# Two chained matmuls with a gelu between them: half of the first and the whole of the second from seven half-size products each, five of the seven in float32r

## The chip, the cores and the metric

One core of one Trainium2 chip. The metric is the time of one execution in microseconds on the device. Runs come with a state, slow or fast, from their clock and their time. A kernel is always timed beside runs of the kernel before on the same chip.

Names: PE is TensorE (PEld its weight loads), DVE is VectorE, ACT is ScalarE.

## The reference

```python
m, k, n, p = 1024, 1024, 2048, 1024          # a: m x k, b: k x n, c: n x p, all float32
h = np.matmul(a, b)
h = 0.5 * h * (1 + np.tanh(np.sqrt(2 / np.pi) * (h + 0.044715 * h ** 3)))
return np.matmul(h, c).astype(np.float32)
```

## The kernel before

It holds h transposed (hT, with n on the partitions), so that the second matmul can take it as weights. a is turned by TensorE. The rows of a come in two halves, aT[0] and aT[1], of 512 columns each. Everything is bf16 and accumulates in float32 banks of 128 x 512.

```python
# opening: k-slices of a's early half and of b's first 768 columns, as they land
for k in range(KT):
    ...                                       # cast, four transposes, copy to aT[0][:, k]
    if k > 0:
        mm0(k - 1)                            # six tiles, accumulated over k
mm0(KT - 1)
...
def mm1(t, h):                                # one tile of hT: 8 matmuls, then the gelu
    p = ppool.tile([128, H], F32, name="ps")
    for k in range(KT):
        nc.tensor.matmul(p, b_sb[:, k, ts(t, 128)], aT[h][:, k, :],
                         start=(k == 0), stop=(k == KT - 1))
    gelu(t, h, p)
...
for mt in range(MT):                          # second matmul: 16 matmuls a tile, copy, store
    ...
        for t in range(NT):
            nc.tensor.matmul(p, hT[h][:, t, ts(j, 128)], c_sb[:, t, ds(q0, w)], ...)
        store(mt, q0, w, p)
```

## Time and profile before

| what | value |
|---|---|
| median of 3 runs at the time of the prediction | 133.43 us |
| span in the profile | 130.9 us |
| matmuls of 128 x 128 x 512 (or the same in halves) | 512 |
| their pace, bf16 | 0.2158 us at 512 columns, 0.109 at 256 |
| TensorE / VectorE / ScalarE busy | 91% / 16% / 21% |

The prediction shows how these are read: TensorE is full, the other two engines stand idle. One view it does not show is the list of waits (engine and line, what it waited for, us in total, times, longest), here for TensorE in the kernel before:

```profile
PE pt L94 <- DVE ab L91: 3.9, 4, 1.9
PE pt L149 <- DMA ab<-in_a_dram: 2.3, 1, 2.3
...
PE ps L127 <- DMA b_sb<-in_b_dram: 0.4, 1, 0.4
```

After the opening TensorE waits only 2.7 us in all, for loads. Nothing in the kernel before makes it wait for VectorE or ScalarE once the opening is over.

### The profile page before, as it was taken

The numbers are of one execution on the slowest core, as the hardware profiler recorded it, in microseconds if no ns is written. First come the engines' busy times: TensorE is split into PE (matmuls) and PEld (weight loads), VectorE is DVE, ScalarE is ACT, GpSimd is POOL, SyncE is SP. The second block draws the span as 40 slices with busy tenths as digits, with TensorE's granted clock in tenths as the row PEclk, the third lists the DMA queues.
The fourth block names the chain that finished last, engine by engine and source line by source line (L and its number), as shares of the span: only waits on it lengthen the run. The fifth ranks groups of instructions, "written<-read, shape, count | busy, mean of one in ns | idle before, by whom it ended". The sixth has DMA issues, their size and how long they took to land.

```text
span 130.9 us, 1420 instructions
## 1 busy us (share of the span) xinstructions
PE 119.2 (91%) x591; PEld 56.3 (43%) x602; DVE 21.0 (16%) x38; ACT 27.2 (21%) x50; POOL 14.6 (11%) x27
## 2 busy tenths in 40 slices
PE   6856899998299999999999999999999999999990
PEld 2323444443155444444444444444444444444570
DVE  0223451000042200000000022222222222211121
ACT  4045556516111333333333100000000000000000
POOL 2000099232462000000000000000000000000000
PEclk9999999999999999999999999999999999999999
DMA  3999999999999999950000022221111222222231
GB/s 110 201 367 380 378 236 168 179 202 205 209 211 210 211 212 211 211 112 1 0 0 0 5 80 80 80 78 59 60 59 69 80 80 80 80 80 80 80 120 40
DMA packets 12196, 17.37 MB, mean 133 GB/s; under 512 B 800, under 2 KB 6688, under 8 KB 12192
## 3 DMA queue, kind: packets, MB, share of 16 engines
q0 software_dynamic: 5952, 7.87, 34.8%
q1 hardware_dynamic: 6240, 9.44, 20.8%
q8 instruction: 4, 0.07, 0.2%
HBM read 20.97 MB, written 4.19 MB: 192 GB/s over the span
## 4 chain that ended last, share of the span: by engine, by line
PE 70%; DMA 18%; POOL 5%; SPq 4%; issue 1%; DVE 0%
PE ps L171 42%; PE ps L127 26%; DMA ab<-in_a_dram 10%; DMA b_st<-in_b_dram 7%; POOL b_sb L110 4%; SPq L66 3%; PE pt L149 1%; SPq L60 1%; DVE ot L163 0%; POOL gate L75 0%
## 5 line engine op out<-in xcount | busy, mean ns | idle before, releaser
L171 PE MATMUL ps<-c_sb,hT 128*128 128x512 bf16 (+1 forms) x267 | 55.2, 367 | 0.3
L127 PE MATMUL ps<-aT,b_sb 128*128 128x512 bf16 x172 | 38.8, 379 | 0.6 <-DMA b_sb<-in_b_dram 0.4
L171 PEld LDWEIGHTS <-hT 128*128 128x128 bf16 x272 | 26.6, 98 | 28.9
L127 PEld LDWEIGHTS <-b_sb 128*128 128x128 bf16 x176 | 16.9, 98 | 20.5 <-DMA b_sb<-in_b_dram 0.9
L103 ACT ACTIVATE hT<-ps 128x512 bf16<-128x512 f32 x30 | 17.3, 602 | 30.0 <-PE ps L127 27.7
L163 DVE COPY ot<-ps 128x512 f32<-128x512 f32 (+1 forms) x17 | 11.2, 660 | 73.2 <-PE ps L171 73.2
L86 PE MATMUL ps<-aT,b_sb 128*128 128x512 bf16 x47 | 11.5, 379 | 0.1
L97 ACT ACTIVATE b_sb<-b_st 128x384 bf16<-128x384 f32 x16 | 7.5, 515 | 10.7 <-DMA b_st<-in_b_dram 10.5
L94 PE MATMUL pt<-ident,ab 128*128 128x128 bf16 x32 | 3.4, 233 | 3.9 <-DVE ab L91 3.9
L137 POOL DMA_DIRECT2D c_sb<-in_c_dram x8 | 5.7, 714 | 6.9 <-DMA b_sb<-in_b_dram 4.7
L86 PEld LDWEIGHTS <-b_sb 128*128 128x128 bf16 x48 | 4.4, 98 | 4.0
L150 DVE COPY aT<-pt 128x1024 bf16<-128x1024 bf16 x4 | 2.8, 692 | 20.5 <-PE pt L149 20.5
L110 POOL DMA_DIRECT2D b_sb<-in_b_dram x8 | 6.0, 775 | 0.0
L80 PE MATMUL pt<-warm 128*128 128x512 bf16 x10 | 4.5, 632 | 1.2 <-DVE warm L46 1.2
L94 PEld LDWEIGHTS <-ab 128*128 128x128 bf16 x32 | 2.3, 104 | 6.9 <-DVE ab L91 5.8
L118 PE MATMUL ps<-aT,b_sb 128*128 128x512 bf16 x16 | 4.8, 379 | 0.1
L118 PEld LDWEIGHTS <-b_sb 128*128 128x128 bf16 x32 | 3.1, 98 | 3.8
L91 DVE CAST ab<-a_st 128x512 bf16<-128x512 f32 x8 | 3.6, 445 | 6.2 <-DMA a_st<-in_a_dram 6.2
L118 PE MATMUL pt<-aT,b_sb 128*128 128x512 bf16 x15 | 4.5, 379 | 0.0
L149 PE MATMUL pt<-ident,ab 128*128 128x128 bf16 x32 | 2.5, 220 | 2.3 <-DMA ab<-in_a_dram 2.3
L95 DVE COPY aT<-pt 128x512 bf16<-128x512 bf16 x8 | 3.4, 425 | 6.4 <-PE pt L94 6.4
L149 PEld LDWEIGHTS <-ab 128*128 128x128 bf16 x32 | 2.0, 98 | 3.5 <-DMA ab<-in_a_dram 2.8
(13 smaller groups left out, 7.5 us busy)
## 6 DMA issues: line engine op xcount, KB each, us to landing
c_sb<-in_c_dram POOLq DMA_DIRECT2D x8, 512.0 KB, 15.3
out_dram<-ot SPq DMA_DIRECT2D x15, 256.0 KB, 2.0
b_st<-in_b_dram SPq DMA_DIRECT2D x8, 384.0 KB, 8.7
a_st<-in_a_dram SPq DMA_DIRECT2D x3, 512.0 KB, 8.9
b_sb<-in_b_dram POOLq DMA_DIRECT2D x4, 384.0 KB, 11.4
b_sb<-in_b_dram POOLq DMA_DIRECT2D x4, 256.0 KB, 5.9
ab<-in_a_dram POOLq DMA_DIRECT2D x4, 256.0 KB, 13.8
a_st<-in_a_dram SPq DMA_DIRECT2D x2, 256.0 KB, 4.2
```

The lines of the kernel that those rows point to most:

```text
L80: nc.tensor.matmul(wps, warm[:, 0:128], warm, start=True, stop=True)
L86: nc.tensor.matmul(ps[t], b_sb[:, k, ts(t, 128)], aT[0][:, k, :], start=(k == 0), stop=(k == KT - 1))
L94: nc.tensor.transpose(pt[:, ts(j, 128)], ab[:, j, :], ident)
L97: nc.scalar.activation(b_sb[:, k, ts(i, W0 // 2)], b_st[k][:, ts(i, W0 // 2)], AF.Copy)
L103: nc.scalar.activation(hT[h][:, t, :], p, AF.Gelu_apprx_tanh)
L110: nc.gpsimd.dma_start(out=b_sb[:, k0:k0 + kn, ds(n0, w)], in_=bv[:, k0:k0 + kn, ds(n0, w)])
L118: nc.tensor.matmul(ps[t], b_sb[:, k + i, ds(W0 + t * 128, 128)], aT[0][:, k + i, :], start=(k + i == 0), stop=(k + i == KT - 1))
L127: nc.tensor.matmul(p, b_sb[:, k, ts(t, 128)], aT[h][:, k, :], start=(k == 0), stop=(k == KT - 1))
L137: nc.gpsimd.dma_start(out=c_sb[:, t0:t0 + 2, :], in_=cv[:, t0:t0 + 2, :])
L149: nc.tensor.transpose(pt[:, k, :], ab[:, ts(k, 128)], ident)
L163: nc.vector.tensor_copy(ot[:, 0:w], p)
L171: nc.tensor.matmul(p, hT[h][:, t, ts(j, 128)], c_sb[:, t, ds(q0, w)], start=(t == 0), stop=(t == NT - 1))
```

## The change

The intent is to do fewer matmuls. A product of 2 x 2 blocks takes eight block products in the plain way and seven in this one, at the price of sums of blocks:

```
S1 = A21+A22  S2 = S1-A11   S3 = A11-A21  S4 = A12-S2
T1 = B12-B11  T2 = B22-T1   T3 = B22-B12  T4 = T2-B21
C11 = A11 B11 + A12 B21                            (products 1 and 2)
V   = A11 B11 + S2 T2       U = V + S3 T3          (products 6 and 7)
C22 = U + S1 T1             C12 = V + S1 T1 + S4 B22        (products 5 and 3)
C21 = U - A22 T4                                   (product 4)
```

The sums are kept in float32r, a four-byte type for TensorE; the operands of products 1 and 2 stay bf16. The first 1024 columns of b are still done plainly (128 matmuls), the others by seven products of 16 matmuls; the second matmul by seven of 32. Below, "the first seven" and "the second seven" are these two. The diff, cut to its core:

```diff
+    class Seven:
+        def dve(self, dst, x, y, op, n=1):            # a sum, in n pieces
+            ...
+                nc.vector.tensor_tensor(out=dst[:, r], in0=x[:, r], in1=y[:, r], op=op)
+        ...
+        def plain(self, n=1):                         # B22 and -A22 as float32r, on ScalarE
+            ...
+    def seven(w, done, between):
+        ...
+        for j in range(4):
+            w.product(px[j], A11, B11, j, True)
+            p1[j] = snap("m", px[j], "p1")            # ScalarE saves the bank
+        between(1)
+        for j in range(4):
+            p = bank(Y[j])
+            w.product(p, A12, B21, j, True)
+            done(0, 0, j, plus(p, p1[j]))             # VectorE adds the saved tile
+        between(2)
+        ...                                           # product 6 onto px -> v; between(6)
+        ...                                           # product 7 onto px -> u; between(7)
+        py = [bank(i) for i in Y]
+        for j in range(4):
+            w.product(py[j], w.s[0], w.t[0], j, True)
+            done(1, 1, j, plus(py[j], u[j]))
+        between(5)
+        for j in range(4):
+            w.product(py[j], w.s[1], w.t[2], j, False)
+            done(0, 1, j, plus(py[j], v[j]))
+        between(3)
+        ...                                           # product 4 onto px
+    def between1(n):                                  # VectorE's sums in the first seven
+        if n == 2:
+            one.s3()
+        elif n == 6:
+            two.s3(2)
+            one.s4()
+            one.t4()
+        elif n == 7:
+            one.plain()
+            two.t1(4)
+        elif n == 5:
+            two.t[1] = slot("x0", [128, 8, H], F32R, "x2")
+            two.t2(4)
+    ...
+    def between2(n):                                  # and in the second
+        if n == 1:
+            two.s1(4)
+        elif n == 2:
+            two.s2(4)
+            two.t3(4)
+        elif n == 6:
+            two.s4(4)
+        elif n == 7:
+            two.plain(4)
+            two.t4(4)
```

Also changed: the opening makes seven tiles in place of six, from slices of 1024 columns of b; a's late half is loaded before b's late half, and its transposes (`turn`) and its product with b's first half come right after the opening, the first four tiles at 256 columns a matmul; 8 warm-up matmuls in place of 10. In the traces here VectorE's instructions stand in the order of the program, so the place of a sum in `between` is its place in VectorE's queue.

## The prediction

> **What bounds the kernel now.** I read the page's table of shares first, then the slices, the groups of instructions with their shapes kept apart, and the chain of work that ended last; after them the timeline of VectorE in the second matmul and of the opening.
>
> ```profile
> span 130.9 us, 1420 instructions
> PE 119.2 (91%) x591; PEld 56.3 (43%) x602; DVE 21.0 (16%) x38; ACT 27.2 (21%) x50; POOL 14.6 (11%) x27
> PE   6856899998299999999999999999999999999990
> DMA  3999999999999999950000022221111222222231
> PE 70%; DMA 18%; POOL 5%; SPq 4%; issue 1%; DVE 0%
> ```
>
> TensorE is full from about 20 us to the end, and it is 70% of the chain; VectorE and ScalarE are busy 16% and 21%. DMA is full until about 58 us of the span and then only stores. The rest of the chain (DMA, POOL, SP queue) is the loading at the front. So only fewer matmuls, or a shorter opening, can make this kernel faster.
>
> ```profile
> L171 PE MATMUL ps<-c_sb,hT 128*128 128x512 bf16 x235 | 51.7, 379 | 0.3
> L163 DVE COPY ot<-ps 128x512 f32<-128x512 f32 x15 | 10.4, 692 | 70.8 <-PE ps L171 70.8
> L171 PE MATMUL ps<-c_sb,hT 128*128 128x256 bf16 x32 | 3.7, 273 | 0.0
> L163 DVE COPY ot<-ps 128x256 f32<-128x256 f32 x2 | 0.8, 424 | 2.4 <-PE ps L171 2.4
> L171 PEld LDWEIGHTS <-hT 128*128 128x128 bf16 x272 | 26.6, 98 | 28.9
> ```
>
> A matmul's 379 ns is a latency, not a pace: the matmuls overlap. The pace stands in the copies, each of which waits for 16 matmuls:
>
> ```profile
> 75.79 0.69 DVE L163 COPY ot<-ps 128x512 f32<-128x512 f32 x1 [32.12 <-PE ps L171]
> 79.24 0.69 DVE L163 COPY ot<-ps 128x512 f32<-128x512 f32 x1 [2.76 <-PE ps L171]
> ...
> 124.14 0.69 DVE L163 COPY ot<-ps 128x512 f32<-128x512 f32 x1 [2.76 <-PE ps L171]
> 125.88 0.42 DVE L163 COPY ot<-ps 128x256 f32<-128x256 f32 x1 [1.05 <-PE ps L171]
> ```
>
> From 75.79 to 79.24 is 3.45 us for 16 matmuls: 0.2158 us each at 512 columns. From 124.14 to 125.88 is 1.74 us for 16 at 256 columns: 0.109 us. The weight load's 98 ns hides in both. The kernel has 512 full-width matmuls, 110.5 us of the span.
>
> [...] I [...] take the 0.2158 us of bf16 for it. No instruction of the kernel before shows this. [...] The trace agrees for copies: 692 minus 424 ns over 256 columns is 1.05 ns[...]. It has no two-tensor operation.
>
> **The change part by part.**
>
> Removed: the first 1024 columns of the first matmul stay as they are (128 matmuls). The other half becomes seven products of 16 in place of 128 (112), the second matmul seven of 32 in place of 256 (224). That is 464 for 512: 48 x 0.2158 = 10.4 us less TensorE work. Two of each seven products stay bf16; five take float32r, in all 5 x 16 + 5 x 32 = 240 matmuls.
>
> The opening: seven tiles in place of six, b in slices of 1024 columns. Up to b's last slice 6.29 MB must land in place of 5.24. Between 9.1 and 16.0 us the kernel before landed 2.62 MB, 378 GB/s, so 1.05 MB more costs 2.8 us; larger packets at the front should give back some 0.7. In the kernel before, the last slice was cast near 20 us and the opening matmuls ended at 22.6, with 48 done. Now the last lands about 21.5 and 56 are done at about 23.8. Eight more matmuls are worth 1.7 us, so this is roughly even. The late half of a is now loaded first, and the wait of 2.3 us for it (and 0.9 us for b) goes. Two waits for the transposed copy (0.69 us each and its hand-over) come. From 23.8: 8 matmuls 1.7, four transposes of a 1.8, 64 at 256 columns 7.0, 32 at 512 6.9, waits 2.0: the plain half ends at T0 = 43.2 us.
>
> Added on VectorE: eight sums a matmul, each with a float32r output[...]. In the first matmul one is 2048 columns: [...] 2.2 us. In the second it is 4096, in four pieces: [...] 4.6 us. An addition of a PSUM tile to a saved one is 512 columns: 0.61 us, 12 of them per matmul. After T0 there remain the sums s3, s4, t4 of the first matmul (6.6), all eight of the second (36), 24 additions (14.6) and the last copies (2): about 60 us of VectorE beside 72.5 us of TensorE (336 x 0.2158). So VectorE is no longer idle, and its order decides. The sums t3, t1, t2 come before b's late half and hide before T0; s1 and s2 end at 43.7.
>
> In the first seven products (3.45 us each), the second product's additions end at T0 + 7.7, as the matmuls do with their last 0.6. Then, in program order, VectorE has s3 2.2, the second matmul's s3 4.4, s4 and t4 4.4, the second matmul's t1 4.6: T0 + 23.3. Only then comes the first addition of product 5, which must free its bank before product 3 may write there: T0 + 24.0. TensorE is ready at T0 + 17.3. **Wait of 6.8 us.** Then the rest of these additions, t2 of the second matmul (4.6) and product 3's additions: T0 + 32.7; the gelus queue behind them on ScalarE (0.5 to 0.6 each), and the banks that the second matmul begins with are free only at T0 + 34.1. TensorE has ended product 4 at T0 + 31.0. **Wait of 3.1 us.** The second seven begin at 77.3.
>
> There, product 6 needs s2, which stands in VectorE's queue behind the additions of product 2 (last at 91.9) and comes in quarters of 1.14 us; TensorE uses a quarter in 0.43. Waits 2.1 + 3 x 0.7 = **4.2 us.** The rest of VectorE's work then fits. Without waits TensorE would end at 43.2 + 72.5 = 115.7; with 6.8 + 3.1 + 4.2 it ends at 129.8. The kernel before had its last matmul end at 127.6 and its span 3.3 us later; the same tail gives a span of 133.1. The median is 2.5 us over the span before (133.43 to 130.9): 135.6. ScalarE gains 24 savings of tiles at about 0.5 us and the plain copies of 1.9 us twice and about 1.0 us eight times, some 24 us, and stays below TensorE.
>
> **The rivals.** First, the saving arrives: the sums hide and the end is 115.7 + 1 + 3.3 + 2.5, about 122.5. For it speak that VectorE's total of 60 us is below TensorE's 72.5, and that somebody placed the sums by hand; the order I worked out would be harmless if the sums took half as long. Against it: outputs of four bytes[...]. In favour of a mild form, a few waits could be shorter than I have them: 128 to 131.
>
> Second, float32r costs more. If its weight load does not hide, each of 240 matmuls grows. At 15 ns that is 3.6 us, of which a part lies in waits that exist anyway: about 138. At 50 ns about 144. At half rate, 240 x 0.216 = 52 us less what the waits swallow: over 170. The 98 ns under 216 speak against, since even a doubled load would fit; that it is a new operand type speaks for.
>
> Third, the clock. The trace's first ten matmuls start 0.43 us apart, half the later pace[...] some 2 us lost. Nearly all of that would lie in the 3.1 us of wait that follows, so the end moves little.
>
> **Range and chances.** The mechanism gives 135.6 if float32r is free. A mild miss of the waits to the good is as likely as a small cost of float32r, so I predict 135.5. Sums of 2.0 or 2.4 us instead of 2.2 move it by about 2 us, the opening by 1, float32r by up to 6: 129.5 to 141. Two per cent are 2.7 us: faster is under 130.8, slower over 136.1. The middle lies just below the upper boundary. Faster 0.16: needs waits under 9 us in all. Same 0.42. Slower 0.42, because float32r can only cost.
>
> **What would show each step.** In the changed profile: product spacing of 3.45 us in float32r as in bf16, from the saves on ScalarE; VectorE's sums of about 2.3 us (2048) and 1.2 us (1024) in the record; an idle time of TensorE near 60 to 67 us put down to VectorE's additions, another near 74 to 77 put down to a gelu, and a broken row near 91 to 97 with matmuls waiting for s2 in quarters; VectorE busy near 75% overall and near 95% between 47 and 77. TensorE's slices should read 9 up to 60 and dip after. Wrong would be: sums at half the time (then 122), float32r matmuls more than 10 ns apart from bf16 (then 138 and up), or the late half of a landing after 25 us, which would shift everything.

## The result, and the profile after

The changed kernel took 139.19 us (median of 4 runs, 137.92 to 139.44) against 133.78 for the kernel before in the same rounds. The ratio is 1.0405, 95% interval 1.0323 to 1.0488: slower. A ratio here is the mean time of one kernel's fast runs over that of the other's of the same rounds, so not quite the quotient of the medians. It takes all four runs of the kernel before as fast; as three of them lie where later sittings have only slow ones, 1.04 is probably too low. Against fast runs alone, in a later sitting, the ratio was 1.052 (after_again, below). The output is correct. Measured again in a later sitting it had 138.98 us.

The head of its page, with the rows of TensorE, VectorE and the granted clock in 40 slices of 3.43 us, and the chain of work that ended last by engine:

```profile
span 137.2 us, 1506 instructions
PE 118.3 (86%) x570; PEld 78.4 (57%) x576; DVE 84.1 (61%) x91; ACT 50.4 (37%) x77; POOL 12.3 (9%) x23
PE   6798899797999999980399899965999999999980
...
DVE  0326443407999089999999950459959963444421
...
PEclk9999999999999999999559999999599999999998
...
PE 75%; DVE 13%; issue 5%; DMA 3%; ACT 2%; DVEq 0%
```

TensorE's row now has a hole at slices 18 and 19, counted from 0 (62 to 68 us), and a dent at 26 and 27; VectorE reads 9 before and across the hole; the clock reads 5, half speed, in two slices at the end of the hole and after it, and in one after the dent. VectorE has entered the chain with 13%. The waits of TensorE in the changed kernel:

```profile
PE ps L188 <- DVE ot L215: 6.2, 1, 6.2
PE ps L188 <- DVE s L151: 2.8, 3, 2.1
...
PE ps L188 <- ACT ot L305: 0.5, 1, 0.5
...
PE ps L188 <- ACT hT L97: 0.3, 1, 0.3
```

L188 is the products, L151 the sums, L215 the additions to saved tiles. VectorE's timeline across the hole (start, duration, instruction, count, and in brackets the idle time before it):

```profile
51.15 2.28 DVE L151 TENSOR_TENSOR x<-b 128x2048 fp32r<-128x2048 bf16 x1
53.35 4.49 DVE L151 TENSOR_TENSOR s<-hT,hT 128x2048 fp32r<-128x2048 bf16 x2
57.76 2.28 DVE L151 TENSOR_TENSOR x<-b,x 128x2048 fp32r<-128x2048 bf16 x1
59.96 2.28 DVE L151 TENSOR_TENSOR x<-x,aT 128x2048 fp32r<-128x2048 f32 x1
62.16 4.62 DVE L151 TENSOR_TENSOR x<-c_sb 128x1024 fp32r<-128x1024 bf16 x4
66.70 2.47 DVE L215 TENSOR_TENSOR ot<-ps,u 128x512 f32<-128x512 f32 x4
69.10 4.62 DVE L151 TENSOR_TENSOR x<-c_sb,x 128x1024 fp32r<-128x1024 bf16 x4
73.64 2.47 DVE L215 TENSOR_TENSOR ot<-ps,v 128x512 f32<-128x512 f32 x4
```

In order these are s3, the second matmul's s3, s4, t4, the second matmul's t1, the additions of product 5, the second matmul's t2, the additions of product 3. VectorE has no idle time here. TensorE is through with product 5 at 61.3; the first of the additions that free its bank is the one at 66.70:

```profile
67.53 9.46 PE L188 MATMUL ps<-x,x 128*128 128x512 f32 x32 [6.19 <-DVE ot L215]
77.31 1.02 PE L188 MATMUL ps<-c_sb,hT 128*128 128x512 bf16 x3 [0.32 <-ACT hT L97]
```

Products 3 and 4 then take 9.46 us; at full clock the same 32 matmuls took 7.42 (in e_best, below). The dent is product 6 of the second seven, which waits for s2 in quarters:

```profile
91.38 0.69 DVE L215 TENSOR_TENSOR ot<-ps,p 128x512 f32<-128x512 f32 x1 [1.03 <-PE ps L188]
91.98 4.62 DVE L151 TENSOR_TENSOR s<-s,hT 128x1024 fp32r<-128x1024 f32 x4
...
93.35 0.70 PE L188 MATMUL ps<-x,s 128*128 128x512 f32 x2 [2.06 <-DVE s L151]
...
94.39 0.73 PE L188 MATMUL ps<-x,s 128*128 128x512 f32 x2 [0.34 <-DVE s L151]
```

Its first tile, eight matmuls, ends at 97.8 having been due to start at 91.2: 6.6 us for 1.8 us of work.

So TensorE got 48 matmuls less, 10.4 us, and lost about 6.2 + 0.3 us at the hole, 2 us there to the clock, 4.8 us at the dent, and to the slower pace of float32r what the experiments measure below.

### The profile page after: what moved, and what is told of

Read it like the earlier page. It is cut to its first block, busy times and chain, and to the rows that moved or that the text cites.

```text
span 137.2 us, 1506 instructions
## 1 busy us (share of the span) xinstructions
PE 118.3 (86%) x570; PEld 78.4 (57%) x576; DVE 84.1 (61%) x91; ACT 50.4 (37%) x77; POOL 12.3 (9%) x23
## 4 chain that ended last, share of the span: by engine, by line
PE 75%; DVE 13%; issue 5%; DMA 3%; ACT 2%; DVEq 0%
PE ps L188 50%; PE ps L124 11%; PE ps L93 10%; DVE x L151 4%; DVE ot L215 3%; DMA sta<-in_a_dram 3%; ACT hT L97 2%; PE pt L85 2%; DVE s L151 2%; DVE aT L120 1%; DVE aT L87 1%; PE pt L119 1%; DVE ab L81 1%; DVE ot L305 0%; ACT ot L305 0%
## 5 line engine op out<-in xcount | busy, mean ns | idle before, releaser
L188 PE MATMUL ps<-x,s 128*128 128x512 f32 (+1 forms) x168 | 39.2, 393 | 3.3 <-DVE s L151 2.8
L188 PEld LDWEIGHTS ps<-x,s 128*128 128x128 f32 x168 | 31.3, 194 | 11.5 <-issue 2.5
L124 PE MATMUL ps<-aT,b 128*128 128x256 bf16 (+1 forms) x102 | 16.0, 312 | 1.8 <-DVE aT L120 1.7
L93 PE MATMUL ps<-aT,b 128*128 128x512 bf16 x55 | 14.4, 416 | 2.1 <-DVE aT L87 2.1
L188 PE MATMUL ps<-x,x 128*128 128x512 f32 x32 | 9.5, 464 | 6.2 <-DVE ot L215 6.2
L188 PE MATMUL ps<-c_sb,hT 128*128 128x512 bf16 x62 | 13.9, 379 | 0.4 <-ACT hT L97 0.3
L124 PEld LDWEIGHTS <-b 128*128 128x128 bf16 x104 | 10.1, 98 | 7.0 <-issue 1.1
L215 DVE TENSOR_TENSOR ot<-ps,p 128x512 f32<-128x512 f32 x8 | 5.5, 692 | 12.7 <-PE ps L188 7.2
L188 PEld LDWEIGHTS ps<-x,x 128*128 128x128 f32 x32 | 7.3, 233 | 8.3 <-issue 6.6
L93 PEld LDWEIGHTS <-b 128*128 128x128 bf16 x56 | 5.9, 105 | 9.4 <-issue 3.0
L188 PE MATMUL ps<-x 128*128 128x512 f32 x48 | 11.3, 393 | 0.0
L188 PEld LDWEIGHTS <-hT 128*128 128x128 bf16 x64 | 6.3, 98 | 8.0 <-issue 0.7
L188 PEld LDWEIGHTS ps<-x 128*128 128x128 f32 x48 | 9.0, 188 | 2.0
L151 DVE TENSOR_TENSOR x<-c_sb 128x1024 fp32r<-128x1024 bf16 x8 | 9.2, 1217 | 0.0
L215 DVE TENSOR_TENSOR ot<-ps,u 128x512 f32<-128x512 f32 x8 | 5.2, 685 | 4.7 <-PE ps L188 2.2
L215 DVE TENSOR_TENSOR ot<-ps,v 128x512 f32<-128x512 f32 x8 | 5.2, 685 | 4.4 <-PE ps L188 4.4
L188 PE MATMUL ps<-aT,b 128*128 128x512 bf16 x31 | 7.0, 379 | 0.1
```

The lines of the kernel that those rows point to most:

```text
L93: nc.tensor.matmul(ps[t], b1[:, k, ts(t, 128)], aT[:, 0, k], start=(k == 0), stop=(k == KT - 1))
L124: nc.tensor.matmul(p[:, ds(m0, w)], b1[:, k, ts(t, 128)], aT[:, h, k, ds(m0, w)], start=(k == 0), stop=(k == KT - 1))
L151: nc.vector.tensor_tensor(out=dst[:, r], in0=x[:, r], in1=y[:, r], op=op)
L188: nc.tensor.matmul(p[:, ds(c0, w)], l[:, k, ts(j, 128)], r[:, k, ds(c0, w)], start=(start and k == 0), stop=(k == self.kt - 1), skip_group ...
L215: nc.vector.tensor_tensor(out=ot, in0=p, in1=st, op=ADD)
```

## The experiments

My theory: the waits come from VectorE's order. It is given the sums of the second matmul while additions that TensorE needs stand behind them. The rivals: VectorE's total is too much, whatever the order; the waits belong to the saves on ScalarE or to the banks; the float32r matmul itself is slow. Twelve kernels ran; all gave a correct result. The table gives them as they were run; the first four, the next four and the last four each shared a chip and its runs of the kernel before.

| run | edit | median us | ratio to before (95%) |
|---|---|---|---|
| e_late_t | two sums later | 133.96 | 1.019 (1.009 to 1.028) |
| e_early_s2 | one sum earlier | 133.55 | 1.018 (1.012 to 1.023) |
| e_both | both | 129.81 | 0.986 (0.976 to 0.996) |
| e_bf16 | changed kernel, bf16 | 124.94 | 0.952 (0.946 to 0.957) |
| e_best | best order | 125.00 | 0.949 (0.945 to 0.953) |
| e_best_warm | and 11 warm-ups | 124.78 | 0.947 (0.944 to 0.951) |
| e_twice_wait | a sum twice | 143.27 | 1.091 (1.084 to 1.098) |
| e_widths | four widths | 140.79 (one run) | |
| after_again | none | 138.98 | 1.052 (1.039 to 1.065) |
| e_twice_free | as much work, elsewhere | 139.93 | 1.058 (1.042 to 1.073) |
| e_best_bf16 | best order, bf16 | 121.67 | 0.923 (0.917 to 0.929) |
| e_best_turns | best order, turns earlier | 123.07 | 0.935 (0.930 to 0.939) |

**e_late_t.** Two sums go behind the additions that TensorE needs.

```diff
         elif n == 7:
             one.plain()
-            two.t1(4)
         elif n == 5:
+            two.t1(4)
+        elif n == 3:
             two.t[1] = slot("x0", [128, 8, H], F32R, "x2")
             two.t2(4)
```

> In the first seven products the second matmul's sum t1 now stands behind product 5's additions in VectorE's queue and t2 behind product 3's. Theory (the waits come from the order of VectorE's queue): the first wait of TensorE, 6.2 us, falls to about 1.7, so no clock drop follows it; the second seven products start about 4.6 us earlier, near 72.7 us; the wait for s2 in quarters stays; time about 134.6 us, ratio to before 1.005. Rival (TensorE waits for the saves on ScalarE or for the banks themselves): no change, 139 us.

133.96 us. The wait for the additions fell from 6.2 to 1.6 us and the second seven started at 72.9 in place of 77.3. Products 3 and 4, behind that wait of 1.6 us, took 7.50 us where the changed kernel has 9.46: no drop of the clock. The profiled run was of state slow (its clock was at half for 6.8 us after the dent, where the changed kernel has 3.4), so its waits are read here only because e_both, in state fast, has the same.

**e_early_s2.** One sum goes ahead of the additions of product 2.

```diff
             two.s1(4)
+            two.s2(4)
         elif n == 2:
-            two.s2(4)
             two.t3(4)
```

> Only the second matmul's s2 moves, ahead of the additions of its product 2. Theory: product 6 of the second matmul no longer waits (2.1 us and three of 0.3 to 0.7 go) and the clock drop near 96 us with them; the first wait stays 6.2 us; time about 134.4 us, ratio about 1.005. Rival (VectorE is simply full, its order does not matter): the wait moves to the additions behind it and the time stays near 139.

133.55 us. The dent is gone: the products in float32r follow in one run, with no bracket of idle time, 35.80 us for the 160 on record (35.78 in e_both). The wait of 6.2 us stays. The expectation held to 0.9 us.

```profile
90.93 35.80 PE L188 MATMUL ps<-x,s 128*128 128x512 f32 x160
```

**e_both.** Both edits.

> Both moves. Theory: the gains add, 4.6 and about 4.8 us: about 130 us, ratio about 0.97. If VectorE's total and not its order were the bound, at most one of the two gains would show: 134 us or more.

129.81 us. From the changed kernel's 139 us, the first edit gave 5, the second 5.5, both 9.2 to 9.4: they add, but for about a microsecond. What is left of the waits for the products in e_both:

```profile
PE ps L188 <- ACT hT L97: 2.3, 1, 2.3
...
PE ps L188 <- DVE ot L215: 1.6, 1, 1.6
```

The 2.3 us for a gelu is the second wait of the prediction, which in the changed kernel had vanished under the slow clock: now products 3 and 4 run at full clock, in 7.52 us, and the wait behind them shows. No total of VectorE stands in the way: it does the same work here.

**e_bf16.** All float32r tiles of the changed kernel become bf16, in the same order.

```diff
-F32R = mybir.dt.float32r
+F32R = mybir.dt.bfloat16
```

> The changed kernel with every float32r replaced by bf16, in the same order (the result may be too inexact; it is for the time). Theory: sums of two bf16 inputs run at twice the rate, 1.2 us for 2048 columns and 0.7 for 1024 in the record; all products have the pace of 3.45 us per 16; the first wait vanishes, the one for s2 shrinks to about 2 us; time about 124 us, ratio about 0.93. If the order alone made the waits whatever a sum costs, about 137.

124.94 us. The groups of sums over c in the changed kernel and, in the second fence, in e_bf16 (count, busy us, mean ns):

```profile
L151 DVE TENSOR_TENSOR x<-c_sb 128x1024 fp32r<-128x1024 bf16 x8 | 9.2, 1217 | 0.0
```

```profile
L151 DVE TENSOR_TENSOR x<-c_sb 128x1024 bf16<-128x1024 bf16 x8 | 5.0, 686 | 0.0
```

Same inputs, only the output narrower: 1217 to 686 ns. By their starts in the two timelines, sums of 2048 columns are 2.20 us apart in the changed kernel and 1.14 in e_bf16, pieces of 1024 columns 1.135 and 0.60. From these I work out 1.04 ns a column with four-byte output and 0.52 with two-byte output, and about 0.07 us for each instruction beside that. So the rate that was expected to double did so with bf16 as output, and not in the changed kernel, where bf16 inputs go into float32r. With sums of that length the same order has no wait at all in the first seven, and one of 1.4 us for s2 is left in the second. So most of the harm needs both, this order and four-byte sums. With four-byte sums the order costs 14 us (139 against e_best's 125.00, below); with two-byte sums it still costs about 3 (124.94 against e_best_bf16's 121.67, in different sittings; 2.0 between the two profiled spans). In bf16, how much exactness is lost was not measured.

**e_best.** I chose the places of the sums by working out, from the durations in the trace, when each engine can start each instruction, for the possible places of each sum.

```diff
-        if n == 2:
+        if n == 1:
             one.s3()
+        elif n == 2:
+            two.t1(4)
         elif n == 6:
-            two.s3(2)
             one.s4()
             one.t4()
         elif n == 7:
             one.plain()
-            two.t1(4)
-        elif n == 5:
+        elif n == 3:
+            two.s3(2)
             two.t[1] = slot("x0", [128, 8, H], F32R, "x2")
             two.t2(4)
```

with the edit of e_early_s2 as well.

> The same work as the changed kernel, in the order that the recurrence of durations finds best: s3 of the first matmul ahead of product 2's additions, the second matmul's t1 right behind them, s4 and t4 next, the second matmul's s3 and t2 behind product 3's additions, s2 ahead of product 2's additions in the second seven. Theory: no wait of TensorE over 0.5 us after 43 us, the last matmul ends near 119.2 us, span 122.6, time about 124.4, ratio about 0.93. If VectorE's total is the bound: 130 or more.

125.00 us, the same work as the changed kernel in 14 us less. One stretch tells it, from 47 to 77 us; the columns are the stretch and its length, busy us and count of PE, PEld, DVE, ACT and POOL, then clock, DMA share and GB/s. The changed kernel first, then e_best:

```profile
47.00:77.00 30.00, 23.75 (x95) 17.82 (x95) 28.53 (x26) 16.40 (x24) 0.00 (x0) 0.89 0.32 61
```

```profile
47.00:77.00 30.00, 30.00 (x137) 20.27 (x135) 28.01 (x27) 20.17 (x31) 0.00 (x0) 1.00 0.31 59
```

VectorE is equally busy in both, 28.5 and 28.0 of 30 us. TensorE is busy 23.75 us in the one and 30.00 in the other, and does 137 matmuls (as recorded) in place of 95. The rival of a full VectorE is out: VectorE was nearly full in both, and in one of them it worked on the right things first.

**e_best_warm.** 11 warm-up matmuls in place of 8.

```diff
-    for _ in range(8):
+    for _ in range(11):
```

> The same with 11 matmuls of warm-up in place of 8. The changed kernel's first 14 opening matmuls took 4.9 us at half clock, the next 14 took 3.2. Theory: at full clock from the first, some 0.6 to 1 us less, about 123.6. Rival (the opening is paced by its loads): no change, 124.4.

124.78 us against 125.00: 0.2 us, less than the 0.6 to 1 expected. In the changed kernel's trace the weight loads of the first opening matmuls start 0.43 us apart from 7.14 to 10.13 us; the first 14 matmuls take 4.88 us, the next 3.18. The clock record of e_best's profiled run has 3.4 us at half clock in the opening (7.3 to 10.7 us), that of e_best_warm none (granted clock over the whole span 0.986 and 0.996), and the first seven began at 43.09 us in place of 43.44. So the slow start costs little here; that the opening is paced by its loads, the rival of the expectation, is not shown.

**e_twice_wait.** The changed kernel, with the sum that I hold to be on the path formed twice.

```diff
             one.plain()
             two.t1(4)
+            two.t1(4)
```

> The changed kernel with the second matmul's t1 formed twice in its place, 4.6 us of VectorE more ahead of product 5's additions. Theory: it lies on the path and the whole of it shows: first wait 10.8 us, time about 143.8. If that wait had another cause, less than 1 us more.

143.27 us, 4.2 above the changed kernel for 4.6 us of added work. TensorE's wait:

```profile
PE ps L188 <- DVE ot L215: 10.7, 1, 10.7
```

It was 6.2: the 4.5 us are all there. (The 4.2 us compares runs in different sittings.)

**after_again** and **e_twice_free.** The second adds the same amount of VectorE work to the changed kernel, behind product 5 of the second seven.

```diff
     def between2(n):
         ...
         elif n == 6:
             two.s4(4)
+        elif n == 5:
+            two.dve(two.x9, two.A[0][0], two.A[1][0], SUB, 4)
```

> The changed kernel itself, unaltered, on the chip of the other runs of this call, so that its ratio stands beside theirs. All theories: 1.04 of before, as in its first measurement.

> The changed kernel with the same amount of extra VectorE work as in the run that formed t1 twice (four two-tensor operations of 1024 columns to float32r, 4.6 us, into a tile that nobody reads), but placed late, behind product 5's additions of the second seven, where VectorE has time. Theory (place in the queue, not the total): no change against the changed kernel, within 0.5 us. Rival (VectorE's total): about 4.5 us slower, as in the other place.

138.98 and 139.93 us. The difference of 0.9 is not clear of noise (the intervals 1.039 to 1.065 and 1.042 to 1.073 overlap), and far from 4.5; it is more than the 0.5 that the expectation allowed. In e_twice_free's timeline the extra sum and what follows it on VectorE:

```profile
119.99 4.62 DVE L151 TENSOR_TENSOR x<-hT,hT 128x1024 fp32r<-128x1024 bf16 x4
124.53 1.88 DVE L215 TENSOR_TENSOR ot<-ps,v 128x512 f32<-128x512 f32 x3
126.58 0.69 DVE L215 TENSOR_TENSOR ot<-ps,v 128x512 f32<-128x512 f32 x1 [0.17 <-PE ps L188]
```

The additions pile up behind it and have caught up with TensorE at 126.58; nobody waits. The profiled run's extra 1.5 us lies earlier, where its half clock after the dent lasted 6.8 us and not 3.4, before the added sum had begun. The same work costs 4.2 us in one place and none that shows in another.

**e_best_bf16.** The best order and bf16 together.

> The best order with every float32r replaced by bf16. With no wait left for sums in either, what remains between the two is the float32r matmul's pace, 240 x 0.011 us = 2.6 us: about 122.3 against 124.9 of the best order, ratio about 0.93. If float32r cost nothing but its sums, no difference.

121.67 us. Without float32r the best order gains 3.3 us, where I expected 2.6. They ran on different chips, so 0.7 us is not much of a difference; neither trace has a wait for a sum. Median distances of matmul starts in the traces: 0.227 us for float32r in e_best, 0.216 for bf16 in both.

**e_widths.** In the changed kernel's second seven, product 7 runs as 256 + 256 columns and product 3 as 384 + 128.

```diff
-            w.product(px[j], w.s[2], w.t[2], j, False)
+            for c0, cw in ((0, H),) if w is one else ((0, 256), (256, 256)):
+                w.product(px[j], w.s[2], w.t[2], j, False, c0, cw)
 ...
-            w.product(py[j], w.s[1], w.t[2], j, False)
+            for c0, cw in ((0, H),) if w is one else ((0, 384), (384, 128)):
+                w.product(py[j], w.s[1], w.t[2], j, False, c0, cw)
```

> In the second seven, product 7 in two halves of 256 columns and product 3 in 384 and 128. It measures the float32r matmul's pace at four widths; at 512 it is 0.2268 us in the changed kernel against 0.2158 in bf16. If a fixed 11 ns comes with each matmul: 0.12 at 256, 0.173 at 384, 0.066 at 128. If the rate per column is 5% lower: 0.115, 0.171, 0.057. If the weight load (188 ns in the record, 98 in bf16) sets a floor: about 0.135 at both 256 and 128, and 0.17 at 384.

The saves on ScalarE follow each tile of product 7, sixteen matmuls of 256 columns:

```profile
107.16 0.60 ACT L210 ACTIVATE u<-ps 128x512 f32<-128x512 f32 x1 [1.32 <-PE ps L188]
109.08 0.60 ACT L210 ACTIVATE u<-ps 128x512 f32<-128x512 f32 x1 [1.32 <-PE ps L188]
```

1.92 / 16 = 0.120 us. The single starts in the trace give 0.227 us at 512 columns, about 0.174 at 384, 0.120 at 256 and 0.111 at 128. Bf16 has 0.216 at 512 and 0.109 at 256. So float32r costs 11 ns more per matmul at 512 and at 256 alike, and the 0.174 at 384 fits the 0.173 that was expected for a fixed amount: a fixed amount at these widths, not a rate. At 128 columns the same rule gave 0.066 us and 0.111 came, where bf16 transposes of 128 columns start 0.056 apart; so the fixed amount alone does not hold there. The record of a weight load is longer in float32r; two groups of the changed kernel:

```profile
L188 PEld LDWEIGHTS ps<-x 128*128 128x128 f32 x48 | 9.0, 188 | 2.0
...
L188 PEld LDWEIGHTS <-hT 128*128 128x128 bf16 x64 | 6.3, 98 | 8.0 <-issue 0.7
```

Whether the 11 ns and the 0.111 us belong to this longer load was not tried.

**e_best_turns.** The best order, 11 warm-ups, and the turns of a's late half one step earlier.

```diff
     turn(0, 0)
-    mm1(p7, 7, 0, range(4, KT))
-    gelu(7, 0, p7)
+    mm1(p7, 7, 0, range(4, 5))
     turn(1, 1)
+    mm1(p7, 7, 0, range(5, KT))
+    gelu(7, 0, p7)
 ...
     for t in range(4):
         mm1(ps[t], t, 1, range(KT), 0, 256)
-    turn(2, 0)
-    turn(3, 1)
+        if t in (1, 2):
+            turn(t + 1, t - 1)
```

> The best order with 11 matmuls of warm-up, and the four turns of a's late half each placed ahead of matmuls that do not need them, so that VectorE's copy of 0.69 us lies beside work. Theory: the two waits of TensorE of 0.9 and 0.8 us for that copy go, about 1.6 us less: 123.1 us. If the late half of a lands too late for the earlier turn, the wait only changes its name: 124.7.

123.07 us, 1.7 less than e_best_warm (on another chip; the ratios 0.935 and 0.947 say the same), as expected. The two waits for the copy are gone from the list. This is the fastest version that keeps float32r, 0.935 of the kernel before; e_best_bf16, at 0.923, is the fastest of all.

## Why the prediction was right or wrong

**The bound and the saving.** Right. TensorE does 48 matmuls less. e_best, where no wait of over 0.5 us is left after 43 us, has about 6.7 us of the 10.4 by its ratio; of the rest, 240 float32r matmuls at 0.011 us more are 2.6.

**The opening and the plain half.** T0 was to be 43.2 us; the first seven started at 43.4. The two waits for the transposed copy came as predicted, at 0.9 and 0.8 us. The 0.7 us for larger packets was an estimate. By 16.0 us the changed kernel had landed 4.84 MB in 2569 packets, the kernel before 4.56 MB in 3492; the 0.28 MB between them are 0.7 us at 378 GB/s. Whether the packets' size made it was not tried.

**The sums.** Right: 2.2 us and 4.6 us were predicted back to back. The timeline has pairs in 4.49 us and four quarters in 4.62. The kernel before has no two-tensor operation, so its trace did not show these two sizes; what it shows is the 1.05 ns a column of a copy, and the sums here came out at 1.04 (e_bf16, above). An addition of a PSUM tile, predicted at 0.61 us, took 0.60 back to back (four of product 5 from 66.70 to 69.10). ScalarE's saves took 0.60 us in the record and not 0.5, its plain copies 1.91 and 1.90, and eight of 0.97. The share of VectorE was misjudged: "near 75% overall" was 61%. The trace has 21.9 us of it before 43.4 us, and with these the predicted 60 after T0 would be 62% of the predicted span of 133.1; between 47 and 77 us the predicted 95% was 28.53 of 30.

**The first wait**, 6.8 us predicted, was 6.2, of the predicted cause: the additions of product 5 behind the second matmul's t1. e_late_t and e_twice_wait shrank and stretched it.

**The second wait**, 3.1 us predicted, was 0.3; yet the second seven began at 77.31, where 77.3 was predicted. That is no luck: VectorE's chain sets this start, and its first addition of product 5, predicted at 43.2 + 23.3 = 66.5, began at 66.70. The third rival named the cause, the clock, with an estimate of 2 us that no trace of the kernel before shows. In the hole, 6.2 us long, the clock fell to half at 64.8 us, 3.5 us after the last product had ended at 61.3, and stayed there until 71.6. Products 3 and 4 took 9.46 us and not 7.42, and those 2 us lay in a wait that was there anyway. In e_both the waits of 1.6 and 2.3 us had no such drop behind them: products 3 and 4 took 7.52 us there, and the 62 matmuls on record for products 1 and 2 of the second seven 13.97 us (13.99 for 64 in e_best, which has no wait before them). So the wait for the gelu was back, with 2.3 us. In the changed kernel's dent, which was partly busy, the clock fell at 95.5 us, after 4.3 us in which four matmuls began, and stayed at half for 3.4 us.

**The dent**, 4.2 us predicted, was 6.6 - 1.8 = 4.8, partly through the clock; e_early_s2 removed it.

**What failed is the step "take the 0.2158 us of bf16 for it".** "It" is the float32r matmul, whose pace, as the prediction says, no instruction of the kernel before shows. It took 0.2268. It can be read from the saves of product 7 in the changed kernel, the first and the last of the four, with 24 matmuls between them:

```profile
105.81 0.60 ACT L210 ACTIVATE u<-ps 128x512 f32<-128x512 f32 x1 [1.21 <-PE ps L188]
...
111.25 0.60 ACT L210 ACTIVATE u<-ps 128x512 f32<-128x512 f32 x1 [1.22 <-PE ps L188]
```

5.44 / 24 = 0.2267 us. The prediction placed the cost of float32r in its second rival and gave it no part in the 135.5. One of its own signs of being wrong, "float32r matmuls more than 10 ns apart from bf16 (then 138 and up)", came true. Over 240 matmuls it is 2.6 us; in the changed kernel only what lies after the first tile of the dent shows in full, 152 x 0.011 = 1.7 us, since the first seven hide theirs in their waits. Two smaller terms were missing: the second drop of the clock, after the dent, where the prediction thought of one after the first gap only (the second tile of product 6 took 2.42 us in place of 1.82, and about half a microsecond lies in the first tile), and the last tile's second half, which waits 0.5 us for ScalarE's copy of the first half. That is 129.8 + 1.7 + 1.1 + 0.5 = 133.1 for the last matmul; it ended at 133.8. I have not placed the remaining 0.7. Against this the time lay 1.8 us above the span and not 2.5, so two errors cancelled in part. The 2.5 set the median of three runs against the span of the profiled one; in all 25 later runs of the kernel before, the time lies 1.9 to 2.2 us above that run's own span, in those of the changed kernel 1.8.

**The whole.** 135.5 us was predicted and 139.19 measured, inside the range of 129.5 to 141. The direction was left open, 0.42 each for "same" and for "slower"; it was slower. The term that, as the prediction said, "can only cost" is 1.7 us of it; without that alone the time would still lie above the 136.1 where slower began. And the boundaries themselves stood on 133.43: against the 131.5 us of the later fast runs even 135.5 would be 3% slower, so the chance given to "same" leaned on a baseline that was probably slow. The mechanism held and the sizes of the float32r pace and of the second clock drop did not.

## What to carry to other kernels

When work is moved from a full engine to an idle one, count the idle engine's time by stretches and in the order of its queue, not by its share of the span: here the order of the same sums made 14 us of difference. Put what another engine is waiting for ahead of what is needed later, and ask of each instruction which buffer it frees. The type that an intermediate was stored in set the cost of making it here: two-byte sums took 0.69 us where four-byte sums took 1.22, and a float32r matmul took 11 ns more, at 512 and at 256 columns.
